# FFN output products of a hybrid decoder layer: sums of weight blocks and differences of token operands made in the first-product stage, kept in DRAM, and loaded ready

## The chip, the cores and the metric

One core of a Trainium2 chip runs the whole layer in one launch. The metric is the device time of an execution in microseconds (us), as the median of several runs. The engines are TensorE (PE, matmuls), VectorE (DVE), ScalarE (ACT), GpSimd (POOL) and SyncE (SP), whose queue issues the transfers spoken of here. Each engine works through its own instructions in a fixed order and waits on semaphores.

## The reference

The layer is two half-step SwiGLU feed-forward networks (FFNs) around a token mixer. The change touches the two FFNs alone.

```python
def swiglu(x, w_in, w_out):
    gate, up = jnp.split(x @ w_in, 2, axis=-1)
    return (jax.nn.silu(gate) * up) @ w_out

h = h + 0.5 * swiglu(rms_norm(h, ffn1_norm[i]), ffn1_w_in[i], ffn1_w_out[i])
h = h + hybrid_mixer(rms_norm(h, mix_norm[i]), ...)
h = h + 0.5 * swiglu(rms_norm(h, ffn2_norm[i]), ffn2_w_in[i], ffn2_w_out[i])
return rms_norm(h, final_norm)[:, N_META:]
```

D_MODEL is 1024, D_FF 2816, SEQ 1024, and 16 meta tokens stand ahead of the sequence, so the first FFN has 1040 columns of tokens and the second 1024. All is float32.

## The kernel before, in words

*Number format.* A float32 product is three matmuls on two-part numbers (`mm3`, L155 to L160: high by high, high by low, low by high). An operand is made by `split` (L135 to L138): ACT casts the high part (L136), then POOL or DVE subtracts it to get the low part (L137).

*Seven products for eight.* Every product of 2 x 2 blocks is done with seven block products (numbered 0 to 6 and run in the order 0, 1, 2, 3, 5, 4, 6), on sums and differences of weight blocks and of token blocks, which the adds to PSUM results turn into the four blocks of the output. The weight sums are four DVE instructions (`pair_weights`, L223, L224, L226, L227).

*First products.* For each f of 22 blocks of 128 D_FF columns, a block of w_in for the gate and one for the up part, both loaded as four 256 KB pieces (`load_half`, L145), are multiplied with the normalised tokens in seven products of two column groups (`hidden`, L277 to L319); f = 0 is done plainly (`hidden_plain`). DVE adds PSUM to kept parts (L284), ACT applies the silu, DVE multiplies gate and up (L287), and for f % 4 < 2 subtracts one result from the other (L290). The two halves are written to `hid_d` in DRAM (L292). 168 matmuls of 260 columns make a period of about 20 us. These stages lie at 60 to 505 us and 2416 to 2855 us of the span.

*Output products.* Four f make a group g, five groups in all; the last two blocks are done plainly behind them. For each group and each half e of the output's columns, four 256 KB blocks of w_out are loaded and `pair_weights` makes the seven weight operands; `output` (L377 to L401) runs seven products of four 260-column chains (or two of 512 in the second FFN), and after each product DVE adds the scaled PSUM to the residual `hT` (L398). The tiles `ps_start_gx`, `mm`, `px` and `rx` are these chains' PSUM banks. The token operands of the next group are made meanwhile by `operand_steps` (L347 to L371), a generator that takes one step after each product: `load_hidden` (L340 to L344) loads the group's hidden values into `lower` and `upper`, L360 makes three differences in two halves each (t2 on DVE, the two that follow on POOL), and `put` splits each of the seven operands in two halves, the low parts of operands 0, 2, 3, 4 on DVE, of 1, 5, 6 on POOL. The low part of a weight operand is made on POOL, that of product 2 on DVE. The stages lie at 505 to 735 us and 2856 to 3082 us.

*Order and buffers.* A scheduler puts each engine's instructions in an order at build time; the text of the program gives the dependencies. Raw weights, their high and their low parts have four buffers each, the big tiles of hidden values (`lower`, `upper`, tag `hid`) two, the small tiles of `hidden` (tag `tmp`) five. SP issues all transfers in its own fixed order.

Of the kernel before, what the change touches and what calls it, by code (L numbers as in the profile page):

```python
# [10 lines left out]
F32 = mybir.dt.float32  # L11
# [5 lines left out]
P = 128  # L17
# [28 lines left out]
def _cut(edges):  # L46
    return [(a, b - a) for a, b in zip(edges, edges[1:])]
# [49 lines left out]
def hybrid_layer(ctx, tc, a):  # L97
# [177 lines left out]
    def ffn(fp, hidp, hT, hn, slots, spare, second, w_in, w_out, hid_d, last_blocks, last_weights, tail, first, w0=None):  # L275

        def hidden(f, ws, order, after):  # L277
            sg, q3, q1, q2 = (fp.tile([P, 2, hn], F32, name=n, tag="tmp", bufs=5) for n in ("sg", "q3", "q1", "q2"))
            chains = [[None, None], [None, None]]
            view = hid_d[f].rearrange("p (g h n) -> p g h n", g=2, h=2)  # L280
            made = [0, 0]

# [39 lines left out]
        def hidden_plain(f, ws):  # L322
            view = hid_d[f].rearrange("p (g h n) -> p g h n", g=2, h=2)
# [13 lines left out]
            for half, x in enumerate((q3, q2)):  # L337
                SP.dma_start(view[:, :, half], x)

        def load_hidden(f):  # L340
            ts = [hidp.tile([P, 8 * hn], F32, name=n, tag="hid", bufs=2) for n in ("lower", "upper")]
            for i, t in enumerate(ts):
                SP.dma_start(t.rearrange("p (f t) -> p f t", f=2), hid_d[f + 2 * i:f + 2 * i + 2].rearrange("f p t -> p f t"))
            return ts  # L344


        def operand_steps(xs, ts, puts):  # L347
            b11, b21, t1, b22 = halves_of(ts)
            t2 = [fp.tile([P, 2, hn], F32, name="t2", tag="tmp", bufs=5) for _ in range(2)]
            part2 = lambda x, k: x[k.start // 2] if x is t2 else x[:, k]  # L350

            def put(i, src):
                eng = V if i in puts else G
                for k in (slice(0, 2), slice(2, 4)):
                    split(part2(src, k), xs[i][0][:, k], xs[i][1][:, k], eng)
                    yield i

            def minus(eng, out, x, y):
                for k in (slice(0, 2), slice(2, 4)):
                    eng.tensor_tensor(out=part2(out, k), in0=part2(x, k), in1=part2(y, k), op=ALU.subtract)  # L360
# [7 lines left out]
            yield from put(3, b11)  # L368
            yield from put(5, b21)
            yield from put(4, t1)  # L370
            yield from put(6, b22)  # L371
# [5 lines left out]
        def output(f, e, xs, steps):  # L377
            def block(fi, dh):
                c0 = (4 * dh + 2 * e) * P
                raw = wtile("wraw")  # L380
                SP.dma_start(raw.rearrange("p (f d) c -> p f (d c)", f=2),
                             w_out[0][(f + 2 * fi) * P:(f + 2 * fi + 2) * P, c0:c0 + 2 * P].rearrange("(f p) c -> p f c", p=P))
                return raw

            raws = [[block(fi, dh) for fi in range(2)] for dh in range(2)]
            chains = [{}, {}]
            for i, (wh, wl) in pair_weights(*raws, FAST[min(f // 4, 1)][e]):
# [16 lines left out]
        ng = NF // 4  # L404
        for f in range(NF):
            if f == 0:
                hidden_plain(f, w0 or plain_weights(w_in))
                second()
                continue
            after = lambda i: None  # L410
            if f == NF - 1:
                steps = operand_steps(slots[0], ts, PUTS[0])
# [5 lines left out]
            if f == NF - 3:  # L418
                ts = load_hidden(0)
        for g in range(ng):  # L420
            steps = operand_steps(slots[(g + 1) % 2], load_hidden(4 * g + 4), PUTS[1]) if g + 1 < ng else iter(())
# [6 lines left out]
        for q in range(4):  # L428
            s = slice(2 * hn * q, 2 * hn * q + 2 * hn)
            raw = fp.tile([P, 2, hn], F32, name="raw", tag="tmp", bufs=5).rearrange("p a n -> p (a n)")  # L430
            SP.dma_start(raw, hid_d[f0 + q // 2][:, 2 * hn * (q % 2):2 * hn * (q % 2 + 1)])
# [99 lines left out]
    hid1_d = tc.dram_tile([NF, P, T], F32, name="hid1_d")  # L531
# [56 lines left out]
    ffn(fp, hidp, hT, HN1, slots, spare, start_differences, a["ffn1_w_in"], a["ffn1_w_out"], hid1_d, MIX3[2:] + MIX3[:2], last_weights1, tail1,  # L588
# [875 lines left out]
    hid2_d = tc.dram_tile([NF, P, SEQ], F32, name="hid2_d")  # L1464

# [29 lines left out]
    ffn(fp, fp, hm, HN2, slots, spare, second2, a["ffn2_w_in"], a["ffn2_w_out"], hid2_d, _cut(range(0, SEQ + 1, 256)), last_weights2, tail2,  # L1495
# [24 lines left out]
```

## Time and profile before

| | us |
|---|---|
| median of 3 runs | 3123.21 (3118.93 to 3125.72) |
| the profiled execution | 3122.52 |
| its span, first to last instruction | 3120.7 |
| PE busy | 2940.9 (94%) |
| DVE busy | 1875.0 (60%) |
| POOL busy | 1665.4 (53%) |
| ACT busy | 1300.9 (42%) |

PE's share is an average over stages. The granted clock of PE, 0.969 in the mean, is the share of the higher of its two levels (2.4 and 1.2 GHz) that the records show. Where the text gives a time without "long", it is a point of the span in us. A number in brackets in a row of the timeline is the idle time of that engine just before, with what ended it.

### The profile page before, as it was taken

The page shows a single profiled execution, that of the slowest core. Times are in us where ns is not written, and L with a number is a line of the kernel's source. Part 1 is how long each engine was busy: PE and PEld are TensorE (multiplying, and loading weights), DVE is VectorE, ACT ScalarE, POOL GpSimd, SP SyncE. Part 2 cuts the span into 40 slices and gives each one's busy share as a digit, 9 for nine tenths or more (in the row PEclk, how much of TensorE's full clock was granted, in tenths as well). Part 3 has the DMA queues.
Part 4 walks back from the last instruction along what each step waited for, and adds up shares of the span by engine and source line. Part 5 has one row for each costly group of instructions (what it writes and reads, how often), then busy time and mean ns, then how long its engine had stood idle before and what let it go on. Part 6 is the DMA issues. An engine that isn't in the chain of part 4 may idle for free. (4 is left out here: it accounts for less than half of the span.)

```text
span 3120.7 us, 55266 instructions
## 1 busy us (share of the span) xinstructions
PE 2940.9 (94%) x21463; PEld 2773.9 (89%) x21463; DVE 1875.0 (60%) x3467; ACT 1300.9 (42%) x2687; POOL 1665.4 (53%) x1419
## 2 busy tenths in 40 slices
PE   7999998999899999988999989999998999999898
PEld 6999998899898899988889889988888999998677
DVE  8444448987755556465656665672438544447976
ACT  4333334333555545443445444453324433334332
POOL 5444447754566556543555445445526544447862
PEclk8999999999999999988999999989999999999999
DMA  2322223313222221211221222144533222223322
GB/s 91 106 79 82 79 77 110 115 49 105 57 62 62 61 57 50 71 41 57 71 54 55 65 71 59 58 141 125 185 110 112 80 91 82 80 80 102 113 64 88
DMA packets 324889, 257.19 MB, mean 82 GB/s; under 512 B 24961, under 2 KB 294530, under 8 KB 324626
## 3 DMA queue, kind: packets, MB, share of 16 engines
q1 hardware_dynamic: 324560, 253.65, 26.9%
q8 instruction: 168, 2.75, 0.4%
q14 instruction: 95, 0.78, 0.1%
q10 hardware_dynamic: 66, 0.02, 0.0%
HBM read 200.12 MB, written 53.49 MB: 81 GB/s over the span
## 5 line engine op out<-in xcount | busy, mean ns | idle before, releaser
L137 POOL TENSOR_TENSOR wl<-wraw,wh 128x512 fp32r<-128x512 f32 x806 | 1088.5, 1358 | 1125.3 <-ACT wh L136 1071.8
L136 ACT CAST wh<-wraw 128x512 fp32r<-128x512 f32 x864 | 535.5, 625 | 1040.5 <-issue 195.2
L983 DVE SCALAR_TENSOR_TENSOR cb<-raw,cw,cb 128x344 f32<-128x344 f32 (+2 forms) x216 | 140.1, 680 | 21.0 <-ACT cb L981 19.7
L158 PE MATMUL ps_gate_mm<-act,wh 128*128 128x344 f32 (+1 forms) x352 | 124.7, 355 | 5.0 <-DVE raw L610 4.4
L159 PE MATMUL ps_gate_mm<-act,wh 128*128 128x344 f32 (+1 forms) x352 | 115.6, 328 | 0.0
L160 PE MATMUL ps_gate_mm<-act,wl 128*128 128x344 f32 (+1 forms) x352 | 115.5, 329 | 0.0
L158 PE MATMUL ps_start_mm<-on,wh 128*128 128x260 f32 x392 | 111.7, 285 | 1.9 <-DVE hT L398 1.4
L158 PE MATMUL ps_ffn_mm<-on,wh 128*128 128x256 f32 (+1 forms) x376 | 111.2, 296 | 1.8 <-ACT wh L136 1.5
L160 PE MATMUL ps_start_mm<-on,wl 128*128 128x260 f32 x392 | 111.1, 283 | 1.8 <-POOL wl L137 1.8
L159 PE MATMUL ps_start_mm<-on,wh 128*128 128x260 f32 x392 | 110.9, 283 | 0.0
L160 PE MATMUL ps_ffn_mm<-on,wl 128*128 128x256 f32 (+1 forms) x376 | 110.2, 293 | 0.7 <-POOL wl L137 0.7
L159 PE MATMUL ps_ffn_mm<-on,wh 128*128 128x256 f32 (+1 forms) x376 | 109.8, 292 | 0.0
L284 DVE TENSOR_TENSOR q<-q,ps_start_px 128x260 f32<-128x260 f32 x42 | 17.7, 422 | 124.7 <-PE ps_start_px L160 124.6
L158 PE MATMUL ps_start_px<-on,wh 128*128 128x260 f32 x308 | 87.8, 285 | 4.0 <-DVE hT L398 2.1
L223 DVE TENSOR_TENSOR wraw<-wraw 128x512 f32<-128x512 f32 x62 | 52.5, 847 | 60.9 <-DMA wraw<-ffn_w_in 44.6
L158 PE MATMUL ps_start_mm<-ox,wh 128*128 128x260 f32 x292 | 84.2, 289 | 4.4 <-ACT ox L136 2.5
L160 PE MATMUL ps_start_px<-on,wl 128*128 128x260 f32 x308 | 88.0, 286 | 0.0
L159 PE MATMUL ps_start_px<-on,wh 128*128 128x260 f32 x308 | 87.8, 285 | 0.0
L159 PE MATMUL ps_start_mm<-ox,wh 128*128 128x260 f32 x292 | 83.6, 286 | 3.6 <-DVE ox L137 3.6
L160 PE MATMUL ps_ffn_px<-on,wl 128*128 128x256 f32 (+1 forms) x284 | 83.8, 295 | 0.8 <-POOL wl L137 0.8
L158 PE MATMUL ps_ffn_px<-on,wh 128*128 128x256 f32 (+1 forms) x284 | 83.5, 294 | 0.7 <-ACT wh L136 0.7
L160 PE MATMUL ps_start_mm<-ox,wl 128*128 128x260 f32 x292 | 83.7, 287 | 0.0
(1661 smaller groups left out, 11082.2 us busy)
## 6 DMA issues: line engine op xcount, KB each, us to landing
wraw<-ffn_w_in SPq DMA_DIRECT2D x176, 256.0 KB
wraw<-w_in SPq DMA_DIRECT2D x168, 256.0 KB
wraw<-ffn_w_out SPq DMA_DIRECT2D x88, 256.0 KB
wraw<-w_out SPq DMA_DIRECT2D x48, 256.0 KB
hid_d<-q SPq DMA_DIRECT2D x44, 260.0 KB
hid_d<-q SPq DMA_DIRECT2D x44, 256.0 KB
gates_d<-raw SPq DMA_DIRECT2D x16, 512.0 KB
wraw<-w_branch_ret SPq DMA_DIRECT2D x32, 256.0 KB
```

What stands on the lines that cost most here:

```text
L136: S.copy(hi, raw)
L137: (eng or G).tensor_tensor(out=lo, in0=raw, in1=hi.bitcast(F32), op=ALU.subtract)
L158: PE.matmul(ps, lhsT=wh, rhs=xh, start=first and i == 0, stop=False, skip_group_check=grow)
L159: PE.matmul(ps, lhsT=wh, rhs=xl, start=False, stop=False, skip_group_check=grow)
L160: PE.matmul(ps, lhsT=wl, rhs=xh, start=False, stop=last and i == n - 1, skip_group_check=grow)
L223: V.tensor_tensor(out=ru[0], in0=ru[0], in1=ru[1], op=ALU.add)
L284: V.tensor_tensor(out=out, in0=out, in1=ps, op=ALU.add)
L983: V.scalar_tensor_tensor(out=c, in0=raw[:, s0 + k:s0 + k + n], scalar=cw[:, 24 * k + ct:24 * k + ct + 1], in1=c, op0=ALU.mult, op1=ALU.add)
```

## The change

Each group's seven token operands and each half's four weight sums are made while the first products run, written to DRAM (`opnd_d`, `sums_d`), and loaded ready in the output stage. In blocks with f % 4 > 1, `hidden` loads two parts of the block f − 2 back into a tile `kept`, makes the three differences (t2 on DVE, b11 and d on POOL) and writes them. In even blocks from 2 to 20, `weight_sums` loads four blocks of w_out, makes the four sums on DVE (L383 to L386, the names `a21`, `a11`, `a12`, `a22`) and writes 1 MB. In the output stage, `load_operands` loads one pair of operands ahead of the pair that is being split, and `output` takes products 0, 1 and 5 from w_out and 2, 3, 4 and 6 from the stored sums. The line numbers of before and after answer to each other so: L284 to L295, L287 to L298, L290 to L301, L398 to L438.

```diff
+        ng = NF // 4
+        hid_d = tc.dram_tile([2, P, 4 * hn], F32, name=f"hid_d{hn}")
+        opnd_d = tc.dram_tile([7 * ng, P, 4 * hn], F32, name=f"opnd_d{hn}")
+        sums_d = tc.dram_tile([2 * ng, P, 16 * P], F32, name=f"sums_d{hn}")
...
         def hidden(f, ws, order, after):
...
+            kept = None
+            if 1 < f <= 4 * ng and f % 2 == 0:
+                sums = weight_sums((f - 2) // 2)
+            if f < 4 * ng and f % 4 > 1:
+                kept = hidp.tile([P, 8 * hn], F32, name="kept", tag="hid", bufs=2).rearrange("p (u n) -> p u n", u=4)
+                for u, i in enumerate((0, 4)):
+                    SP.dma_start(kept[:, u], part_of(f - 2, i))
...
                 if made[half] == 2:
-                    SP.dma_start(view[:, :, half], x)
+                    put_hidden(f, half, x)
+                    if half and kept is not None:
+                        flat = lambda t: t.rearrange("p g n -> p (g n)")
+                        b11, t1, t2, d = (kept[:, u] for u in range(4))
+                        V.tensor_tensor(out=t2, in0=flat(q2), in1=t1, op=ALU.subtract)
+                        SP.dma_start(part_of(f, 2), t2)
+                        G.tensor_tensor(out=b11, in0=t2, in1=b11, op=ALU.subtract)
+                        SP.dma_start(part_of(f, 3), b11)
+                        G.tensor_tensor(out=d, in0=flat(q3), in1=t2, op=ALU.subtract)
+                        SP.dma_start(part_of(f, 5), d)
 
             for i, grp in order:
+                if 1 < f <= 4 * ng and f % 2 == 0 and grp == 0:
+                    next(sums, None)
...
+        def weight_sums(n):
+            w = hidp.tile([P, 8 * hn], F32, name="sums", tag="hid", bufs=2)[:, :16 * P].rearrange("p (i c) -> p i c", i=4)
+            a11, a12, a21, a22 = (w[:, i] for i in range(4))
+            for i, (dh, fi) in enumerate(((0, 0), (0, 1), (1, 0), (1, 1))):
+                SP.dma_start(w[:, i].rearrange("p (f c) -> p f c", f=2), block(4 * (n // 2), n % 2, fi, dh))
+            yield
+            yield
+            yield V.tensor_tensor(out=a21, in0=a21, in1=a22, op=ALU.add)
+            yield V.tensor_tensor(out=a11, in0=a21, in1=a11, op=ALU.subtract)
+            yield V.tensor_tensor(out=a12, in0=a12, in1=a11, op=ALU.subtract)
+            V.tensor_tensor(out=a22, in0=a22, in1=a11, op=ALU.subtract)
+            SP.dma_start(sums_d[n], w.rearrange("p i c -> p (i c)"))
+            yield
...
+        LOADS = ((0, 1), (2, 3), (5, 4), (6,))
...
-            minus(V, t2, b22, t1)
-            yield from put(0, b11)
-            minus(G, b11, t2, b11)
-            yield from put(1, b21)
-            minus(G, b21, b21, t2)
-            yield from put(2, t2)
...
+        def operand_steps(xs, g, t, puts):
+            for n, pair in enumerate(LOADS):
+                ahead = load_operands(g, LOADS[n + 1]) if n + 1 < len(LOADS) else None
+                for u, i in enumerate(pair):
+                    eng = V if i in puts else G
+                    for k in (slice(0, 2), slice(2, 4)):
+                        split(t[:, u, k], xs[i][0][:, k], xs[i][1][:, k], eng)
+                        yield i
+                t = ahead
...
         def output(f, e, xs, steps):
...
+            def weights():
+                for i in (0, 1, 2, 3, 5, 4, 6):
+                    raw = wtile("wraw")
+                    if i in (0, 1, 5):
+                        SP.dma_start(raw.rearrange("p (f d) c -> p f (d c)", f=2), block(f, e, *{0: (0, 0), 1: (1, 0), 5: (1, 1)}[i]))
+                    else:
+                        j = {2: 0, 6: 1, 4: 2, 3: 3}[i]
+                        SP.dma_start(raw.rearrange("p k c -> p (k c)"), sums_d[idx][:, 512 * j:512 * j + 512])
+                    yield i, put_weights(raw, eng=V if i in FAST[min(f // 4, 1)][e] else None)
...
-            for i, (wh, wl) in pair_weights(*raws, FAST[min(f // 4, 1)][e]):
+            for i, (wh, wl) in weights():
```

DVE in the first products, before: an early block of the first FFN, `q` being the kept parts, `sg` the gate.

```order
L284 TENSOR_TENSOR sg<-sg,ps_start_px 128x260 x2
L284 TENSOR_TENSOR q_1416<-q_1416,ps_start_px 128x260
L287 TENSOR_TENSOR q_1416<-q_1416,sg 128x260
L223 TENSOR_TENSOR wraw<-wraw 128x512
L284 TENSOR_TENSOR q_1418<-q_1418,ps_start_mm 128x260
L224 TENSOR_TENSOR wraw<-wraw 128x512
L284 TENSOR_TENSOR q_1416<-q_1416,ps_start_px 128x260
L287 TENSOR_TENSOR q_1416<-q_1416,sg 128x260
```

The same place after, in the block f = 3; `sums` are w_out blocks.

```order
L295 TENSOR_TENSOR sg<-sg,ps_start_px 128x260 x2
L295 TENSOR_TENSOR q_1197<-q_1197,ps_start_px 128x260
L383 TENSOR_TENSOR sums<-sums 128x512
L298 TENSOR_TENSOR q_1197<-q_1197,sg 128x260
L223 TENSOR_TENSOR wraw<-wraw 128x512
L384 TENSOR_TENSOR sums<-sums 128x512
L295 TENSOR_TENSOR q_1199<-q_1199,ps_start_mm 128x260
L224 TENSOR_TENSOR wraw<-wraw 128x512
```

Two of the four weight sums now stand between the addition of product 5 (`q<-q,ps_px`) and the addition of product 4 (`q<-q,ps_mm`).

SP in the same blocks, before: each block's four weight loads and its two writes.

```order
L145 DMA wraw<-ffn_w_in 128x4x128 x4
L292 DMA hid_d<-q_2140 256x1x260
L292 DMA hid_d<-q_2142 256x1x260
L145 DMA wraw<-ffn_w_in 128x4x128 x4
L292 DMA hid_d<-q_2380 256x1x260
```

After, in the block f = 3 (L308, L310, L312 write the differences, L380 loads w_out, L387 writes the sums):

```order
L367 DMA opnd_d_364<-q_1940 128x520
L367 DMA opnd_d_364<-q_1942 128x520
L145 DMA wraw<-ffn_w_in 128x4x128
L308 DMA opnd_d_364<-kept 128x520
L310 DMA opnd_d_364<-kept 128x520
L312 DMA opnd_d_364<-kept 128x520
L145 DMA wraw<-ffn_w_in 128x4x128
L380 DMA sums<-ffn_w_out 128x2x256 x2
L145 DMA wraw<-ffn_w_in 128x4x128
L380 DMA sums<-ffn_w_out 128x2x256 x2
L145 DMA wraw<-ffn_w_in 128x4x128
L387 DMA sums_d_365<-sums 128x2048
```

The four loads of w_out have come between the three writes and the weight loads of the next block.

DVE in the output products, before, in one group of the first FFN (`t` is the difference t2; L223 and L224 are weight sums):

```order
L398 SCALAR_TENSOR_TENSOR hT<-ps_start_mm,hT 128x260
L360 TENSOR_TENSOR t_7407<-upper,lower 128x520
L360 TENSOR_TENSOR t_7408<-upper,lower 128x520
L398 SCALAR_TENSOR_TENSOR hT<-ps_start_px,hT 128x260
L398 SCALAR_TENSOR_TENSOR hT<-ps_start_mm,hT 128x260
L398 SCALAR_TENSOR_TENSOR hT<-ps_start_px,hT 128x260
L398 SCALAR_TENSOR_TENSOR hT<-ps_start_gx,hT 128x260
L398 SCALAR_TENSOR_TENSOR hT<-ps_start_mm,hT 128x260
L398 SCALAR_TENSOR_TENSOR hT<-ps_start_gx,hT 128x260
L398 SCALAR_TENSOR_TENSOR hT<-ps_start_px,hT 128x260
L223 TENSOR_TENSOR wraw<-wraw 128x512
L398 SCALAR_TENSOR_TENSOR hT<-ps_start_mm,hT 128x260
L224 TENSOR_TENSOR wraw<-wraw 128x512
```

After, in the same stage (L438 is the addition to the residual, `opnd` a loaded operand):

```order
L137 TENSOR_TENSOR ox<-opnd,ox 128x520
L438 SCALAR_TENSOR_TENSOR hT<-ps_start_mm,hT 128x260
L438 SCALAR_TENSOR_TENSOR hT<-ps_start_px,hT 128x260
L137 TENSOR_TENSOR ox<-opnd,ox 128x520
L438 SCALAR_TENSOR_TENSOR hT<-ps_start_gx,hT 128x260 x3
L438 SCALAR_TENSOR_TENSOR hT<-ps_start_rx,hT 128x260
L137 TENSOR_TENSOR oe<-opnd,oe 128x520
L438 SCALAR_TENSOR_TENSOR hT<-ps_start_mm,hT 128x260
L438 SCALAR_TENSOR_TENSOR hT<-ps_start_px,hT 128x260
L137 TENSOR_TENSOR oe<-opnd,oe 128x520
L438 SCALAR_TENSOR_TENSOR hT<-ps_start_mm,hT 128x260
```

The differences and the sums are gone from between the additions; the halves of operands that DVE splits stand there alone.

## Rows read from the trace of the kernel before

**Rows 1.** The trace by stretches: from:to, length, busy time of each engine (instructions), granted clock, DMA share, GB/s.

```profile
90.00:480.00 390.00, 389.69 (x3241) 389.10 (x3240) 181.16 (x292) 148.14 (x326) 176.40 (x135) 1.00 0.29 85
485.00:505.00 20.00, 17.45 (x138) 16.61 (x137) 16.56 (x18) 9.07 (x21) 18.72 (x12) 1.00 0.21 65
505.00:735.00 230.00, 210.70 (x1666) 206.18 (x1665) 198.49 (x375) 79.21 (x137) 156.39 (x105) 0.97 0.29 92
2440.00:2840.00 400.00, 399.35 (x3347) 399.15 (x3346) 182.47 (x302) 155.08 (x341) 186.60 (x143) 1.00 0.29 86
2840.00:3082.00 242.00, 221.07 (x943) 173.52 (x943) 197.59 (x249) 84.55 (x151) 171.70 (x114) 0.96 0.28 91
665.00:735.00 70.00, 70.00 (x587) 70.00 (x586) 51.75 (x119) 15.99 (x26) 30.12 (x24) 1.00 0.21 62
```

**Rows 2.** Waits from 505 to 735 us: line waiting, releaser, us in total, times, longest.

```profile
PE ps_start_gx L158 <- DVE hT L398: 8.6, 6, 2.7
...
PE ps_start_mm L158 <- DVE hT L398: 3.7, 6, 1.2
```

**Rows 3.** Timeline of PE: start, us, line, operation; in brackets the idle time before and its releaser.

```profile
555.22 0.39 PE L158 MATMUL ps_start_px<-on,wh 128*128 128x260 f32 x1 [0.92 <-DVE hT L398]
...
556.92 0.39 PE L158 MATMUL ps_start_mm<-on,wh 128*128 128x260 f32 x1 [1.19 <-DVE hT L398]
```

**Rows 4.** Timeline of DVE, the same microseconds.

```profile
553.36 1.47 DVE L223 TENSOR_TENSOR wraw<-wraw 128x512 f32<-128x512 f32 x1
...
555.09 1.43 DVE L137 TENSOR_TENSOR ox<-lower,ox 128x520 fp32r<-128x520 f32 x1
```

**Rows 5.** Shorter stretches, columns as in the first group.

```profile
505.00:665.00 160.00, 140.70 (x1081) 136.18 (x1080) 146.75 (x258) 63.22 (x111) 126.27 (x82) 0.96 0.33 105
...
505.00:520.00 15.00, 12.80 (x99) 11.95 (x98) 15.00 (x25) 9.26 (x18) 10.86 (x7) 1.00 0.65 213
580.00:595.00 15.00, 14.79 (x124) 14.58 (x123) 14.70 (x28) 7.34 (x13) 10.04 (x7) 1.00 0.11 36
```

**Rows 6.** DVE's groups, 485 to 735 us: count | busy us, mean ns | idle before.

```profile
L360 DVE TENSOR_TENSOR t<-upper,lower 128x520 f32<-128x520 f32 x9 | 11.1, 1265 | 1.4 <-DMA upper<-hid_d 1.4
L223 DVE TENSOR_TENSOR wraw<-wraw 128x512 f32<-128x512 f32 x10 | 10.7, 1071 | 9.8 <-DMA wraw<-ffn_w_out 9.7
L224 DVE TENSOR_TENSOR wraw<-wraw 128x512 f32<-128x512 f32 x10 | 10.2, 1017 | 0.0
...
L226 DVE TENSOR_TENSOR wraw<-wraw 128x512 f32<-128x512 f32 x10 | 8.9, 892 | 0.1
...
L227 DVE TENSOR_TENSOR wraw<-wraw 128x512 f32<-128x512 f32 x10 | 7.6, 759 | 0.0
```

**Rows 7.** POOL's groups in the same stretch.

```profile
L360 POOL TENSOR_TENSOR lower<-t,lower 128x520 f32<-128x520 f32 x10 | 16.7, 1673 | 0.0
L360 POOL TENSOR_TENSOR upper<-upper,t 128x520 f32<-128x520 f32 x10 | 16.1, 1607 | 0.7 <-DVE t L360 0.7
```

**Rows 8.** The view of line L226: ns shortest/median/longest, first and last start, form.

```profile
L226 DVE TENSOR_TENSOR wraw<-wraw x62: 676/1443/1794, 71.6 to 3060.6; 128x512 f32<-128x512 f32 x62
```

**Rows 9.** Timeline of DVE in one period of first products.

```profile
278.54 1.33 DVE L287 TENSOR_TENSOR q<-q,q 128x260 f32<-128x260 f32 x1 [1.03 <-ACT q L316]
...
282.63 0.43 DVE L284 TENSOR_TENSOR sg<-sg,ps_start_px 128x260 f32<-128x260 f32 x1 [2.41 <-ACT sg L302]
289.55 0.43 DVE L284 TENSOR_TENSOR q<-q,ps_start_px 128x260 f32<-128x260 f32 x1 [6.50 <-PE ps_start_px L160]
...
291.56 0.69 DVE L223 TENSOR_TENSOR wraw<-wraw 128x512 f32<-128x512 f32 x1 [1.12 <-DMA wraw<-ffn_w_in]
292.17 0.42 DVE L284 TENSOR_TENSOR q<-q,ps_start_mm 128x260 f32<-128x260 f32 x1
```

**Rows 10.** Timeline of PE there.

```profile
293.60 0.28 PE L158 MATMUL ps_start_mm<-ox,wh 128*128 128x260 f32 x1
```

**Rows 11.** SP's own waits from 100 to 500 us.

```profile
SPq L343 <- DMA hid_d<-q: 1.6, 1, 1.6
```

More of the change, by code (lines that the diff above doesn't have):

```diff
@@ L273, in plain_weights, with ffn @@
         return [put_weights(r) for rs in raw_pair(cols(w_in, 0), cols(w_in, DFF)) for r in rs]
-    def ffn(fp, hidp, hT, hn, slots, spare, second, w_in, w_out, hid_d, last_blocks, last_weights, tail, first, w0=None):
+    def ffn(fp, hidp, hT, hn, slots, spare, second, w_in, w_out, last_blocks, last_weights, tail, first, w0=None):
+        ng = NF // 4
+        hid_d = tc.dram_tile([2, P, 4 * hn], F32, name=f"hid_d{hn}")
+        opnd_d = tc.dram_tile([7 * ng, P, 4 * hn], F32, name=f"opnd_d{hn}")
+        sums_d = tc.dram_tile([2 * ng, P, 16 * P], F32, name=f"sums_d{hn}")
         def hidden(f, ws, order, after):
@@ L337, in hidden_plain @@
             for half, x in enumerate((q3, q2)):
[L338 to L360, printed above, removed]
-            minus(V, t2, b22, t1)
-            yield from put(0, b11)
-            minus(G, b11, t2, b11)
-            yield from put(1, b21)
-            minus(G, b21, b21, t2)
-            yield from put(2, t2)
[L368 to L371, printed above, removed]
@@ new lines, in hidden_plain, with part_of, put_hidden, block @@
+                put_hidden(f, half, x)
+        def part_of(f, i):
+            return opnd_d[7 * (f // 4) + i][:, 2 * hn * (f % 2):2 * hn * (f % 2 + 1)]
+        def put_hidden(f, half, x):
+            if f < 4 * ng:
+                SP.dma_start(part_of(f, (1, 6)[half] if f % 4 > 1 else (0, 4)[half]), x.rearrange("p g n -> p (g n)"))
+            else:
+                SP.dma_start(hid_d[f - 4 * ng].rearrange("p (g h n) -> p g h n", g=2, h=2)[:, :, half], x)
+        def block(f, e, fi, dh):
+            c0 = (4 * dh + 2 * e) * P
+            return w_out[0][(f + 2 * fi) * P:(f + 2 * fi + 2) * P, c0:c0 + 2 * P].rearrange("(f p) c -> p f c", p=P)
@@ new lines, in ffn, with load_operands @@
+        LOADS = ((0, 1), (2, 3), (5, 4), (6,))
+        def load_operands(g, pair):
+            t = hidp.tile([P, 8 * hn], F32, name="opnd", tag="hid", bufs=2).rearrange("p (u k n) -> p u k n", u=2, k=4)
+            for u, i in enumerate(pair):
+                SP.dma_start(t[:, u].rearrange("p k n -> p (k n)"), opnd_d[7 * g + i])
+            return t
+        def operand_steps(xs, g, t, puts):
+            for n, pair in enumerate(LOADS):
+                ahead = load_operands(g, LOADS[n + 1]) if n + 1 < len(LOADS) else None
+                for u, i in enumerate(pair):
+                    eng = V if i in puts else G
[3 more added lines that the diff above has]
+                t = ahead
@@ L377, in output @@
         def output(f, e, xs, steps):
[L378 to L385, printed above, removed]
+            idx = 2 * (f // 4) + e
+            def weights():
[3 more added lines that the diff above has]
+                        SP.dma_start(raw.rearrange("p (f d) c -> p f (d c)", f=2), block(f, e, *{0: (0, 0), 1: (1, 0), 5: (1, 1)}[i]))
+                    else:
+                        j = {2: 0, 6: 1, 4: 2, 3: 3}[i]
+                        SP.dma_start(raw.rearrange("p k c -> p (k c)"), sums_d[idx][:, 512 * j:512 * j + 512])
+                    yield i, put_weights(raw, eng=V if i in FAST[min(f // 4, 1)][e] else None)
             chains = [{}, {}]
-            for i, (wh, wl) in pair_weights(*raws, FAST[min(f // 4, 1)][e]):
+            for i, (wh, wl) in weights():
                 chain = i in (1, 3, 5)
@@ L417, in ffn @@
             hidden(f, dict(ffn_weights(w_in, f)), first if f == 1 else order, after)
-            if f == NF - 3:
-                ts = load_hidden(0)
+            if f == NF - 2:
+                ts = load_operands(0, LOADS[0])
         for g in range(ng):
-            steps = operand_steps(slots[(g + 1) % 2], load_hidden(4 * g + 4), PUTS[1]) if g + 1 < ng else iter(())
+            steps = operand_steps(slots[(g + 1) % 2], g + 1, load_operands(g + 1, LOADS[0]), PUTS[1]) if g + 1 < ng else iter(())
             for e in range(2):
@@ L1493, in tail2 @@
             SP.dma_start(a["out"][0][t * P:(t + 1) * P, :], ot)
[L1495 removed]
+    ffn(fp, fp, hm, HN2, slots, spare, second2, a["ffn2_w_in"], a["ffn2_w_out"], _cut(range(0, SEQ + 1, 256)), last_weights2, tail2,
         [(i, e) for i in (0, 1, 2, 3, 5, 4, 6) for e in (1, 0)], w0)
```

11 lines of the change are left out of this document (3 added, 8 removed).

## The prediction, made before the changed kernel had run

> **What bounds the kernel now.** I first read busy time by stretch, to see where TensorE (PE) is not working. In the FFNs' first products it is busy for 389.69 of 390 us and 399.35 of 400 us at full granted clock [rows 1]: there is nothing to win there, only something to lose. In the two output stages it is not: from 485 to 735 us PE is busy 17.45 of 20 and 210.70 of 230 us, from 2840 to 3082 us 221.07 of 242 us. That is 2.55 + 19.30 + 20.93 = 42.8 us of idle time. The granted clock is also below 1.00 there, 0.97 over 230 us and 0.96 over 242 us: 6.9 + 9.7 = 16.6 us in which work advanced at the 1.2 GHz level instead of 2.4. Together **59.4 us** is all that the change can return.
>
> Who is late there? PE's waits in the output stage are nearly all for the PSUM additions of L398 on VectorE (DVE): 8.6 us on gx, 3.7 us on mm [rows 2]. The timeline shows why. At 555.22 and 556.92 PE starts after 0.92 and 1.19 us of idle, each released by an addition; ahead of each addition, in DVE's queue, stands something else of 1.4 us: a sum of weight blocks (553.36, L223), then the low part of half an operand (555.09, L137) [rows 3, 4]. So PE waits for a short addition behind long SBUF work, and DVE is busy 146.75 of the 160 us from 505 to 665 [rows 5]. In the last two groups, where no operand is split any more, DVE is busy for 51.75 of 70 us, and PE never stops although the sums L223 to L227 are still made there [rows 1]. What stops PE is therefore the pile on DVE, not the sums as such.
>
> **The change part by part.**
>
> *Removed from the output stages.* Of DVE, in 485 to 735 us: 11.1 us of differences (L360) and 10.7 + 10.2 + 8.9 + 7.6 = 37.4 us of sums; of POOL: 16.7 + 16.1 = 32.8 us of differences [rows 6, 7]. The second FFN has the same instructions on 512-column blocks, as many again. From the 160 us that carry operands go all 11.1 us and about two thirds of the sums, 25 us: DVE falls from 147 to about 111 us. Fewer POOL operations also make what stays cheaper: the same sum takes 676 ns or 1443 ns, median 1443 [rows 8], and the long ones are those beside POOL's work.
>
> How much of the 59.4 us comes back? All of it if DVE is never late, which the last two groups show at a DVE share of 51.75/70 = 74%. DVE's 111 us in a stage cut to some 135 us is 82%, between that and the 92% of before; and from 580 to 595 us DVE is busy 14.70 of 15 us with PE at 14.79 [rows 5], so even a full DVE need not stop PE where additions stand between the long operations, as they do in the changed order (only halves of operands, with one to four additions between two of them, where two differences stood in a row and sums after single additions). I take 80%: **−48 us**. Bounds: −59.4, and −30 if the splits of operands alone (one of the two waits in [rows 3, 4]) keep half of the loss.
>
> *Added to the first products*: the same number of instructions on each compute engine, so all that left the output stages is now beside products that leave no gap. Per FFN, ten blocks f make t2 (DVE) and b11, d (POOL), and ten make four sums on DVE; SP gets 310 more transfers. Engine time is there: DVE is busy 181.16 of 390 us and POOL 176.40 [rows 1]; DVE's 48.5 us and POOL's 33 us raise both to under 60%. What costs is place, in order queues.
>
> (a) *Sums in the blocks f = 3, 7, 11, 15, 19* (five per FFN). In a period of before (286 to 299 us) DVE adds product 5 at 289.55, waits 1.12 us for the weights (L223 at 291.56), and at 292.17 adds product 4's PSUM, to 292.6 [rows 9]; PE starts product 6 in that PSUM at 293.60 [rows 10]. The slack is 1.0 us. In the changed order L383, which waits for weight loads of its own, stands between the first of these and all the others, and L384 too stands ahead of the addition. When do its blocks land? Their buffer is the one that t2, b11 and d are written from, so they wait for these three writes. t2 can be made when the block's last gating has ended, at 278.54 + 1.33 = 279.9 in this period [rows 9], then 1.3 us; b11 and d follow on POOL with 1.6 to 1.7 us each [rows 7] between pairs of weight splits: d is ready at some 286.5 us. From there the queue has to move the write of d, the four loads and the weights between them, about 7 x 256 KB = 1.84 MB. The fastest stretch of the trace moved 213 GB/s at a share of 0.65 [rows 5], 328 GB/s if full: 5.6 us, to 292.1. Even before, with four transfers in that time, DVE waited until 291.56 for the weights [rows 9]. L383 of 0.7 to 1.4 us, L298, L223 and L384 then put the addition's end at 294.5 to 297 instead of 292.6, against a limit of 293.6: 1 to 3.5 us late. I take 2 us, ten times: **+20 us** (0, if the loads are there by 291; 40, if each also meets the longer sums and a landing 2 us later).
>
> (b) *Sums in f = 1, 5, 9, 13, 17*: loaded in time, but four in a row between the two gate additions, 4 x 0.68 to 4 x 1.44 us [rows 8]. Between these two additions DVE idles 2.41 us, to 282.63 [rows 9], which nearly covers 2.7 us and leaves 3.4 us of 5.8; the second one frees a PSUM bank that PE's product 3 needs. I take 0.7 us ten times: **+7** (0 to 20).
>
> (c) At the start of each FFN the first loads stand ahead of the next block's weights on SP: about one transfer of 256 KB each, **+2** (0 to 6).
>
> (d) t2 on DVE in front of the next block's gate addition, b11 and d on POOL in front of weight splits: POOL has 214 us of gaps in 390 [rows 1], over 10 us of each block. **0** (to 5).
>
> (e) *Transfers in the output stage*: operands come ready made, seven a group of 512 or 520 KB instead of two loads of 1 MB, so some 7.3 MB per group (with 3.5 MB of weights) instead of 4.1 (2 + 2): in some 40 us 185 GB/s. The trace moved 213 at 0.65 busy [rows 5], so the queue holds it, and a pair is asked for one pair (some 11 us) ahead: **0** (to 15, one late pair per group).
>
> A load of kept operands needs what an earlier block wrote. The trace has one such wait on SP, 1.6 us in the first products of the first FFN [rows 11], where nothing close reads what was just written; the new loads read a block two back, some 40 us old. The Trainium skill (DMA: Bandwidth & Descriptors, "Rules for kernel authors") has a dependent transfer issued only after the first one's completion, on the same queue too. By this rule SP stands still when a write is slow, and all later weight loads with it: it speaks against the change, and is what the third rival prices from rows.
>
> Sum: −48 + 20 + 7 + 2 = −19 us against the profiled execution's 3122.5 us (span 3120.7 us): 3103.5; it lies 0.7 us below the median of the runs, 3123.2, so **3104 us**.
>
> One rule makes the gain doubtful from the other side: the long sums. The median 1443 against 676 ns [rows 8] appear wherever POOL works on SBUF. The Trainium skill (SBUF — State Buffer, "Who interferes with whom") has DVE and GpSimd share one pair of ports under an exclusive lock. By it a sum costs as much in its new place, and the sum above would only move within the range of (b).
>
> **The rivals.**
>
> 1. *The loads land in time* (first products keep their 389.69 of 390). For it: DMA share there is 0.29 [rows 1]; against it: the slack of 1.0 us. Gain −48, costs 0 to 2: **3076 us**. Chance 0.20.
>
> 2. *DVE stays the bound of the output stage*: operand halves and additions, which all remain, keep half the loss: −30, and first products cost 29: **3122 us**, no change. For it: one of the two waits in [rows 3, 4] stands behind half an operand. Against: 580 to 595 us. Chance 0.18.
>
> 3. *SP and DVE hold each other up in the first products*, slower. If L383's loads come 2 us later than in (a), because SP waits for the three writes and holds the next weights too, each of the ten late blocks loses 4 us and each of the ten early ones 2: +60 + 2, and with −48 it is +14; with a gain of −42 it is +20. It decides from 4.8 us lost in each late block without any other loss. **3140 us**. For it: seven transfers between d and the sum, against four before; against it, that the share of 0.29 leaves room. Chance 0.14.
>
> 4. *It does not do what it says*: the counts of instructions per engine are equal before and after, so work is moved, not saved; if DVE in the output stage were not the limit (PE waiting for weights) nothing would return. PE's largest waits are not for weights [rows 2]. Chance 0.03, 3135 us.
>
> **How the numbers follow.** My forecast, costs in part as large as in (a) and (b), 3090 to 3115 us: 0.45. This kernel's measurement can tell some 0.2% (6 us) from no change: faster is below 3117, slower above 3129.5. Faster: 0.45 + 0.20 and a small part of rival 2, 0.67. Within: most of rival 2, 0.16. Slower: rivals 3 and 4, 0.17. The range reaches from 3068 (rival 1 with a little less than the full 59.4 back) to 3133 (between rivals 2 and 3); left out are the full gain at no cost, and rival 3 at its price.
>
> **What would show it.** Right: in the output stages PE busy over 97% with the clock at 0.99; waits for the line of the PSUM addition below 4 us; in the first products gaps of about 2 us every fourth block, released by the addition of product 4's PSUM behind L383, with DVE waiting for a transfer. Without such gaps rival 1 holds; with DVE over 90% busy in the output stage and PE waiting as before, rival 2; with gaps of 4 us and more that end in weights from SP, rival 3. Wrong altogether would be idle PE in the output stages that ends in operand transfers.

## The result, and the profile after

The changed kernel takes 3145.43 us (median of 4 runs, 3144.29 to 3146.3) against 3121.07 us before (4 runs, 3111.08 to 3125.72): a ratio of 1.0082, 95% interval 1.006 to 1.0103. It is 0.8% slower. I had forecast 3104 us and a range of 3068 to 3133 us.

Where the time went is told by the stages. First products run from their first addition in the trace (L284 before, L295 after) to the first addition of the output products (L398, L438), and these to the end of their last addition on gx.

| stage, us | before | after | difference |
|---|---|---|---|
| first products, FFN 1 | 427.2 | 461.8 | +34.6 |
| output products, FFN 1 | 229.1 | 205.7 | −23.4 |
| between the two | 1695.6 | 1692.5 | −3.1 |
| first products, FFN 2 | 426.3 | 470.3 | +44.0 |
| output products, FFN 2 | 226.5 | 197.8 | −28.7 |

Stage times here and below are those of one profiled execution of each kernel. The output stages gave back 52.1 us. The first products took 78.6 us. With the 3.1 us between the two that makes 23.4, the difference of the two spans (3144.0 and 3120.7 us). The view by stretches of the changed kernel (columns as in [rows 1]):

```profile
90.00:480.00 390.00, 367.60 (x2971) 363.38 (x2970) 190.84 (x315) 134.75 (x301) 185.84 (x143) 0.98 0.46 149
...
545.00:735.00 190.00, 186.33 (x1539) 184.68 (x1537) 147.58 (x303) 69.12 (x121) 115.47 (x82) 1.00 0.51 169
2440.00:2840.00 400.00, 371.58 (x2983) 366.69 (x2984) 184.24 (x317) 136.70 (x307) 192.66 (x144) 0.97 0.46 147
2908.00:3106.00 198.00, 194.75 (x849) 157.26 (x848) 140.10 (x188) 74.79 (x132) 118.22 (x87) 1.00 0.52 173
```

In the output stages PE is now busy for 186.33 of 190 us at a full clock, where it was 210.70 of 230 at 0.97. In the first products it is busy for 367.60 of 390 us, where it was 389.69, and the granted clock there is 0.98 and 0.97 where it was 1.00. DMA moves 149 GB/s where it moved 85. What PE waits for in FFN 1, from 60 to 545 us and then from 545 to 746 us:

```profile
PE ps_start_mm L158 <- DVE q L295: 20.9, 12, 3.8
PE ps_start_px L158 <- DVE sg L295: 7.8, 6, 1.9
```

```profile
PE ps_start_mm L158 <- DVE hT L438: 2.1, 2, 1.9
PE ps_start_gx L158 <- DVE hT L438: 1.5, 4, 0.5
```

The wait for the residual's additions has fallen from 8.6 and 3.7 us [rows 2] to 1.5 and 2.1. A wait for the addition of product 4's PSUM has come, 20.9 us. The longest of these gaps, on PE, DVE, SP and POOL:

```profile
226.04 0.39 PE L158 MATMUL ps_start_mm<-ox,wh 128*128 128x260 f32 x1 [3.85 <-DVE q L295]
```

```profile
217.98 0.43 DVE L295 TENSOR_TENSOR q<-q,ps_start_px 128x260 f32<-128x260 f32 x1 [6.50 <-PE ps_start_px L160]
223.41 0.69 DVE L383 TENSOR_TENSOR sums<-sums 128x512 f32<-128x512 f32 x1 [5.00 <-DMA wraw<-ffn_w_in]
224.02 0.42 DVE L298 TENSOR_TENSOR q<-q,sg 128x260 f32<-128x260 f32 x1
224.36 0.69 DVE L223 TENSOR_TENSOR wraw<-wraw 128x512 f32<-128x512 f32 x1
224.96 0.68 DVE L384 TENSOR_TENSOR sums<-sums 128x512 f32<-128x512 f32 x1
225.56 0.42 DVE L295 TENSOR_TENSOR q<-q,ps_start_mm 128x260 f32<-128x260 f32 x1
```

```profile
211.71 0.32 SPq L312 DMA_DIRECT2D opnd_d<-kept  x1
212.96 0.38 SPq L145 DMA_DIRECT2D wraw<-ffn_w_in  x1
216.12 0.90 SPq L380 DMA_DIRECT2D sums<-ffn_w_out  x2
217.12 0.42 SPq L145 DMA_DIRECT2D wraw<-ffn_w_in  x1
217.59 1.01 SPq L380 DMA_DIRECT2D sums<-ffn_w_out  x2
218.64 0.47 SPq L145 DMA_DIRECT2D wraw<-ffn_w_in  x1
```

```profile
211.64 2.54 POOL L137 TENSOR_TENSOR wl<-wraw,wh 128x512 fp32r<-128x512 f32 x2
```

Read from below. POOL has freed the weight buffers by 214.2 us, but SP stands from 213.3 to 216.1 at L380, whose buffer is held by the write L312; so the third weight load leaves only at 217.12. Six transfers of 256 KB then leave within 3 us. DVE waits for the last of them until 223.41 with L383 at the head of its queue, and the addition that PE needs comes at 225.56. PE is idle for 3.85 us. And then, in the stretches around the gap:

```profile
218.00:222.00 4.00, 4.00 (x35) 3.98 (x34) 0.41 (x1) 0.62 (x1) 0.49 (x2) 1.00 0.94 294
222.00:224.00 2.00, 0.19 (x2) 0.00 (x0) 0.59 (x1) 0.00 (x0) 1.15 (x1) 1.00 0.38 114
224.00:226.00 2.00, 0.00 (x0) 0.00 (x0) 2.00 (x6) 0.00 (x0) 0.00 (x0) 1.00 0.00 0
226.00:228.00 2.00, 1.96 (x10) 1.96 (x11) 2.00 (x4) 0.62 (x1) 0.64 (x1) 0.59 0.00 0
228.00:230.00 2.00, 2.00 (x12) 2.00 (x12) 2.00 (x5) 0.39 (x1) 0.93 (x1) 0.55 0.76 319
230.00:232.00 2.00, 2.00 (x18) 2.00 (x18) 0.76 (x2) 0.00 (x0) 0.00 (x0) 1.00 0.86 342
```

The DMA engines are 0.94 busy from 218 to 222 us, while DVE waits and PE still works; from 224 to 226 us, while PE waits for DVE, they move nothing. For 4 us after the gap the granted clock is 0.59 and 0.55, which is 1.7 us more. Ten and twelve matmuls run in 2 us where eighteen do a moment later.

The period shown is the extreme one. Such a gap stands in ten blocks, five in each FFN, and it is 3.1 to 3.9 us long in all of them, but SP's wait at L380 is 2.7 us only here and 0.9 us in the mean of the other four blocks of FFN 1 (waits of SP from 60 to 545 us):

```profile
SPq L292 <- DMA opnd_d<-q: 39.1, 18, 4.3
...
SPq L380 <- DMA opnd_d<-kept: 6.4, 5, 2.7
```

Another of the ten, on SP and DVE, with its gap on PE:

```profile
397.36 0.37 SPq L145 DMA_DIRECT2D wraw<-ffn_w_in  x1
```

```profile
398.35 0.43 DVE L295 TENSOR_TENSOR q<-q,ps_start_px 128x260 f32<-128x260 f32 x1 [6.50 <-PE ps_start_px L160]
401.99 0.69 DVE L383 TENSOR_TENSOR sums<-sums 128x512 f32<-128x512 f32 x1 [3.22 <-DMA wraw<-ffn_w_in]
...
405.21 0.41 DVE L295 TENSOR_TENSOR q<-q,ps_start_mm 128x260 f32<-128x260 f32 x1
```

```profile
405.68 0.39 PE L158 MATMUL ps_start_mm<-ox,wh 128*128 128x260 f32 x1 [3.13 <-DVE q L295]
```

The same load before:

```profile
288.57 0.37 SPq L145 DMA_DIRECT2D wraw<-ffn_w_in  x1
```

Before, the last weight load left 1.0 us ahead of product 5's addition (289.55 [rows 9]), the first sum began 3.0 us after the load had left (291.56), and product 4's addition began 0.6 us after that. Here the load left 1.0 us ahead too, but the first sum began 4.6 us after it, and product 4's addition 3.2 us after that, behind L383, L298, L223 and L384. In the mean of the ten blocks product 4's addition comes 4.5 us later than before: 0.6 us because the last weight load leaves later, 1.6 us because it lands more slowly (read from the start of the sum that waits for it), and 2.4 us by what stands on DVE between the first sum and the addition.

### The profile page after: what moved, and what is told of

Its sections match the earlier page's. It is cut to its first block, busy times and chain, and to the rows that moved or that the text cites. A ratio compares the mean times of both kernels' runs of the same rounds, so it can differ in the third digit from the quotient of the medians.

```text
span 3144.0 us, 55888 instructions
## 1 busy us (share of the span) xinstructions
PE 2940.9 (94%) x21463; PEld 2779.0 (88%) x21463; DVE 1832.4 (58%) x3467; ACT 1291.0 (41%) x2687; POOL 1641.1 (52%) x1419
## 5 line engine op out<-in xcount | busy, mean ns | idle before, releaser
L298 DVE TENSOR_TENSOR q<-q,q 128x260 f32<-128x260 f32 (+1 forms) x84 | 63.6, 757 | 55.7 <-ACT q L338 55.7
L158 PE MATMUL ps_ffn_mm<-ox,wh 128*128 128x256 f32 (+1 forms) x264 | 77.6, 294 | 17.1 <-DVE q L295 16.9
```

The source lines that it names most:

```text
L158: PE.matmul(ps, lhsT=wh, rhs=xh, start=first and i == 0, stop=False, skip_group_check=grow)
```

## The experiments

Two theories stood against each other. **H**: a sum that waits for its loads stands on DVE ahead of PSUM additions. **T**, later **C**: the weights of the first products themselves come late, because other transfers stand ahead of them on SP and on the DMA engines; the first sum of these weights, L223, also stands ahead of product 4's addition. All ratios are to the kernel before, run on the same chip in turn. First products are given as FFN 1 / FFN 2, in us.

**The sums on DVE left out.** The edit removes the four DVE instructions and keeps their loads and their write.

```diff
-            yield V.tensor_tensor(out=a21, in0=a21, in1=a22, op=ALU.add)
-            yield V.tensor_tensor(out=a11, in0=a21, in1=a11, op=ALU.subtract)
-            yield V.tensor_tensor(out=a12, in0=a12, in1=a11, op=ALU.subtract)
-            V.tensor_tensor(out=a22, in0=a22, in1=a11, op=ALU.subtract)
+            yield
```

> The changed kernel without the four sums on DVE (L383 to L386); their loads and writes and everything else stay, so product operands 2, 3, 4 and 6 of the weights are unsummed blocks. In the changed kernel the first products last 461.8 us (FFN1) and 470.3 us (FFN2) where they lasted 427.2 and 426.3. Theory H (a sum that waits for its loads stands in DVE's queue ahead of PSUM additions): the stalls go, 428 to 434 us each, total 3066 to 3080 us. Theory T (the added transfers, 152 against 85 GB/s, make the weights of the first products late by themselves): stays at 455 to 470 us each, total above 3130 us.

Measured: 3124.74 us, ratio 1.0014 (1.000 to 1.0028); first products 449.2 / 454.8. Neither theory alone: 28 of the 78.6 us went, 50 stayed. (The profiled execution is the fastest of ten, 12 us below the median; by the medians some 21 us went.) DVE at one of the gaps that stayed:

```profile
212.35 0.43 DVE L295 TENSOR_TENSOR q<-q,ps_start_px 128x260 f32<-128x260 f32 x1 [6.50 <-PE ps_start_px L160]
...
218.23 0.69 DVE L223 TENSOR_TENSOR wraw<-wraw 128x512 f32<-128x512 f32 x1 [4.99 <-DMA wraw<-ffn_w_in]
218.84 0.42 DVE L295 TENSOR_TENSOR q<-q,ps_start_mm 128x260 f32<-128x260 f32 x1
```

No sum stands here, and DVE waits the same 5 us: now L223 waits, for weights, where it waited 1.12 us before [rows 9].

**Each half of the change alone.** First the operand differences, with `pair_weights` back in the output stage; then the weight sums alone, with `load_hidden` and the differences as before.

```diff
-            for i, (wh, wl) in weights():
+            for i, (wh, wl) in pair_weights(*raws, FAST[min(f // 4, 1)][e]):
```

> The operand differences are moved as in the change, the weight sums are made in the output stage as before. Theory H: first products as before, 427 to 431 us each; the output stages (229.1 and 226.5 us before, 205.7 and 197.8 changed) get back about a third to a half of 52 us, since 11 us of DVE and 33 us of POOL leave each but 37 us of sums stay on DVE: total 3095 to 3108 us. Theory T: the three writes and two loads of the kept parts make a part of the stalls, first products 440 us or more each, total 3120 us or more.

Measured: 3089.05 us, ratio 0.9903 (0.9887 to 0.9919); first products 427.7 / 432.6, output stages 216.3 / 201.7. The differences alone cost 7 us in the first products, 6 of them in FFN 2, and give back 37.6 us, more than the expected third to half of 52.

> Only the weight sums are moved, as the change moves them; operands and differences are as before. Theory H: sums wait for their loads in DVE's queue here too, but no write of differences holds their buffer, so the stalls are smaller than in the changed kernel: first products 435 to 455 us each; output stages give back some 30 us together: total 3105 to 3140 us. Theory T: the sums' 2 MB per two blocks are most of the added traffic, so first products are as in the changed kernel, 455 to 470 us each, total 3150 us.

Measured: 3119.72 us, ratio 0.9993 (0.9978 to 1.0008); first products 431.3 / 435.5, output stages 222.8 / 216.9. The sums alone cost 13 us and give 16: no change. So the halves cost 7 and 13 us in the first products, and together 78.6: what makes the loss is that they meet. Alone, each has the two big buffers and SP to itself; together, a load of one waits in SP's queue for a write of the other, as L380 does above. These two runs do not show that this is the reason; the next ones move the queues' order.

**The sums moved on DVE.** All work and all transfers of the change, but the four sums are pinned behind the second gate addition of the odd block.

```diff
                     add(sg[:, grp], ps)
                     S.activation(sg[:, grp], sg[:, grp], AF.Silu)
+                    if f % 2 and grp and sums:
+                        next(sums.pop())
...
+                tc.keep_in_program_order(V.tensor_tensor(out=out, in0=x, in1=y, op=op))
```

> The changed kernel with one thing moved: the sums of an even block are made one block later, in DVE's queue behind the second gate addition of the odd block, where DVE waits 6.5 us for PE; their loads are issued in the even block as before, some 20 us ahead of their use. All work and all transfers stay. Theory H: first products 428 to 440 us each (what is left comes from weights that SP issues late behind the new waits), total 3070 to 3090 us. Theory T: as the changed kernel, 455 us or more each, total above 3130 us.

Measured: 3131.23 us, ratio 1.0041 (1.0028 to 1.0054); first products 451.4 / 462.1. Theory H alone falls: with no sum in the way, DVE waits 47.2 us for weights in FFN 1 from 90 to 480 us (21.8 us before), and the same group of loads stands between the weight loads on SP.

**The w_out loads behind the same block's weights.** The kernel above, with the four loads pinned on SP.

```diff
-                SP.dma_start(w[:, i].rearrange(...), block(4 * (n // 2), n % 2, fi, dh))
+                tc.keep_in_program_order(SP.dma_start(w[:, i].rearrange(...), block(4 * (n // 2), n % 2, fi, dh)))
```

> As the kernel with the sums moved behind the second gate addition (first products 451.4 and 462.1 us), and in addition SP issues the four w_out loads of a block behind the four weight loads of that block, so that in every fourth block they no longer stand between these. Theory C (weights of the first products come late because other transfers stand ahead of them on SP and on the DMA engines, and DVE's first sum of these weights, L223, stands ahead of product 4's PSUM addition): the gaps of 2.4 to 2.7 us once in four blocks go, first products 435 to 446 us each, total 3095 to 3115 us; the loads of kept parts still stand ahead of two weight loads in another of four blocks. Theory H (only sums on DVE hold PE up): no change against 451 and 462, total 3131 us.

Measured: 3105.16 us, ratio 0.995 (0.9933 to 0.9967); first products 438.9 / 445.2. Theory C as expected: in FFN 1 the gaps of 2.2 to 2.7 us once in four blocks are gone, and gaps of 0.6 to 1.8 us stay, mostly in another of four blocks.

**Small transfers.** The kernel without sums on DVE, with loads of 32 of 256 columns and a write of 32 of 512; the output stage loads blocks of w_out in place of the stored ones.

```diff
-                SP.dma_start(w[:, i].rearrange("p (f c) -> p f c", f=2), block(...))
+                SP.dma_start(w[:, i].rearrange("p (f c) -> p f c", f=2)[:, :, :32], block(...)[:, :, :32])
```

> As the kernel without the sums on DVE (first products 449.2 and 454.8 us), and in addition the four loads of w_out and the write in the first products carry 32 of 256 columns, with the same waits on SP in the same places; the output stage takes unsummed blocks of w_out in place of the stored ones. Two forms of theory C: if bytes are what makes the weights late, first products fall to 428 to 434 us each and the total to 3070 to 3080 us; if SP's wait for the writes that hold the shared buffer is it, 440 us or more each remain and the total stays above 3100 us. With a part by each, 434 to 440 us.

Measured: 3104.81 us, ratio 0.9951 (0.9936 to 0.9965); first products 444.6 / 445.1. SP and the stretches at one gap:

```profile
211.23 0.42 SPq L145 DMA_DIRECT2D wraw<-ffn_w_in  x1
211.70 1.01 SPq L380 DMA_DIRECT2D sums<-ffn_w_out  x2
214.73 0.53 SPq L386 DMA_DIRECT2D sums_d<-sums  x1
215.30 0.63 SPq L145 DMA_DIRECT2D wraw<-ffn_w_in  x1
```

```profile
214.00:216.00 2.00, 2.00 (x19) 2.00 (x18) 0.00 (x0) 0.00 (x0) 0.00 (x0) 1.00 0.05 8
216.00:218.00 2.00, 1.18 (x10) 0.97 (x9) 0.00 (x0) 0.62 (x1) 1.12 (x1) 1.00 0.71 157
```

From 214 to 216 the DMA engines are 0.05 busy, and still the last weight load leaves only at 215.30: SP stands at the write L386 until its four loads have landed. So waits in SP's queue alone make weights late. The totals do not price the bytes: with small transfers the scheduler put L386 ahead of the last weight load, behind which it stands in the kernel without the sums, and this is a wait of its own, so 444.6 may not be set against 449.2 as a share. The timelines show what the bytes do: in the ten late blocks the first sum begins 3.1 to 4.1 us after the last weight load has left, against 4.9 to 6.0 us in the kernel without the sums, where the transfers have their full size.

**Everything behind the next block's weights.** Work and transfers as in the change. The next block's four weight loads are written ahead of the middle of this block; the loads of kept parts, the loads of w_out and the write of the sums are pinned behind them on SP, and the sums on DVE as above.

```diff
+                if i == 3 and grp == order[-2][1]:
+                    if f + 1 < NF:
+                        raws.append(raw_pair(cols(w_in, (f + 1) * P), cols(w_in, DFF + (f + 1) * P)))
+                    if f % 2 and sums:
+                        next(sums.pop())
...
+                            tc.keep_in_program_order(SP.dma_start(kept[:, u], part_of(f - 2, j)))
...
+            tc.keep_in_program_order(SP.dma_start(sums_d[n], w.rearrange("p i c -> p (i c)")))
```

> All work and all transfers of the changed kernel, but the loads of kept parts, the loads of w_out and the write of the sums stand on SP behind all four weight loads of the next block, and the four sums stand on DVE behind the second gate addition of the odd block. Theory C: first products 428 to 436 us each, output stages 205 and 198 us as in the changed kernel, total 3068 to 3085 us, faster than the kernel with the operand differences alone (3089 us). If the bytes as such are too many (150 against 85 GB/s), first products stay at 445 us or more and the total above 3110 us.

Measured: 3080.66 us, ratio 0.987 (0.9856 to 0.9885), faster than both kernels and than the differences alone; first products 428.2 / 430.4, output stages 209.8 / 197.5. SP in one period, and the stretches of the first products:

```profile
221.33 4.41 SPq L145 DMA_DIRECT2D wraw<-ffn_w_in  x3
225.79 2.04 SPq L387 DMA_DIRECT2D sums<-ffn_w_out  x4
```

```profile
90.00:480.00 390.00, 388.07 (x3211) 385.97 (x3210) 224.40 (x333) 146.40 (x324) 209.99 (x155) 1.00 0.51 166
...
2440.00:2840.00 400.00, 397.64 (x3305) 394.59 (x3303) 227.36 (x345) 154.93 (x342) 217.26 (x160) 1.00 0.52 171
```

The weight loads leave with nothing between them, and the loads of w_out after them. DMA moves 166 and 171 GB/s, more than the 149 and 147 of the changed kernel, and PE is busy for 388 of 390 us. The bytes were never too many; their place was wrong.

**The same, with the sums where the scheduler wants them on DVE.** This takes the pin from the four sums and nothing else.

```diff
-                tc.keep_in_program_order(V.tensor_tensor(out=out, in0=x, in1=y, op=op))
+                V.tensor_tensor(out=out, in0=x, in1=y, op=op)
```

> As the kernel with all added transfers behind the next block's weights on SP (first products 428.2 and 430.4 us, total 3080.7 us), but the four sums are put on DVE where the scheduler wants them: in the first FFN at the end of the block whose middle issued their loads, ahead of the last addition of product 4. So weights come on time and only the sums' place on DVE is bad again. Theory H as a second cause of its own: DVE waits 2 to 5 us for w_out blocks in front of that addition, ten times in each FFN, first products 445 to 470 us each, total 3110 to 3160 us. If only the weights' lateness mattered (theory C alone): as before the edit, 428 to 434 us each, 3080 to 3088 us.

Measured: 3115.3 us, ratio 0.9991 (0.9977 to 1.0006); first products 455.0 / 441.4. DVE at one place:

```profile
215.70 0.69 DVE L223 TENSOR_TENSOR wraw<-wraw 128x512 f32<-128x512 f32 x1 [3.25 <-DMA wraw<-ffn_w_in]
...
218.01 0.41 DVE L291 TENSOR_TENSOR q<-q,ps_start_px 128x260 f32<-128x260 f32 x1
...
242.94 0.90 DVE L390 TENSOR_TENSOR sums<-sums 128x512 f32<-128x512 f32 x1 [0.81 <-DMA sums<-ffn_w_out]
243.76 0.41 DVE L291 TENSOR_TENSOR q<-q,ps_start_mm 128x260 f32<-128x260 f32 x1
```

```profile
218.57 0.36 PE L158 MATMUL ps_start_px<-ox,wh 128*128 128x260 f32 x1 [0.89 <-DVE q L291]
...
220.82 0.48 PE L158 MATMUL ps_start_mm<-on,wh 128*128 128x260 f32 x1 [1.03 <-DVE q L291]
```

The edit costs 27 and 11 us, and the total came out as theory H expected, but not by its mechanism. A sum does stand ahead of product 4's addition (242.94), with a wait for w_out of 0.8 us and not of 2 to 5; but PE does not stop there: after 220.82 its next stop is 0.48 us at 248.57. Its stops for additions are at 218.57 and 220.82 and at the same places in every fourth block of FFN 1, where no sum of w_out is in the way. There the order of other instructions has changed with the pin: L223, which waits 3.25 us for the weights, and L224 stand ahead of both additions of product 5, where both stood behind the first of these in the kernel above. In FFN 1's first products PE's idle time is 17.5 us against 5.8, and the granted clock is 0.98 from 90 to 480 us where it was 1.00 in the run above; the two make up most of the 27 us. So this run does not show the place of the sums as a cause by itself. What shows it is the run without the sums, and a row from the start of FFN 2 in the next section.

Along the kernels with the same work and the same transfers, the sums moved on DVE return 18.6 of the 78.6 us, the w_out loads behind the same block's weights another 29.4, and all added transfers behind the next block's weights another 25.5: 73.5 in all. What remains is 5 us.

## Why the prediction was wrong, step by step

- **The bound, and what the output stages return.** Right. 48 us of 59.4 forecast, 52.1 measured, by the mechanism named: the wait for the residual's additions went, the clock rose to 1.00. Its makeup was not as I had it: I reckoned mostly with the sums (37 of 48 us of DVE), but the differences alone give 37.6 us and the sums alone 16. DVE's 11 us of differences and POOL's 33 us weigh more than 37 us of sums, which [rows 1] had hinted at: in the last groups the sums are made and PE does not stop.
- **(a), the sums in every fourth block.** This term failed by its size: 20 us forecast, 34 us of gaps measured. The place was right: the gap is on product 6, behind the addition of product 4, behind L383. I took 2 us of gap, and it is 3.1 to 3.9 us in each of the ten blocks. The step in it that was wrong: "from there the queue has to move ... 5.6 us, to 292.1", which is 2.5 us after product 5's addition. Measured, the first sum began 3.6 to 5.4 us after it, 4.1 in the mean. I had seen that the loads wait for the writes, but let the weights behind them go out as before. In the period shown first, SP stood 2.8 us at L380 and the last weight load left 1.6 us later than before; in the mean of the ten it left 0.6 us later, and it landed 4.6 us after it had left, not 3.0. What follows on DVE I had listed rightly: 1 to 3.5 us late was my bracket, and I took 2 where 3.4 came. (The 213 GB/s from which I had the 328 were not the fastest of the trace, which moved 349 GB/s from 2102 to 2117 us; the rate is not what failed.)
- **The clock.** This term was put at nothing, without a reason, though I had counted the clock among the gains. The gap of 3.85 us is followed by 4 us at 0.59 and 0.55. Over 390 and 400 us a clock of 0.98 and 0.97 is 7.8 + 12 = 20 us, as much as I had set for all of (a). (The 16.6 us among the gains are what the clock cost; the time at the lower level was twice that. The sum does not change.)
- **(b), the early sums.** Right in size, 5.5 us of gaps against 7, but not as described: "loaded in time" was wrong. From 258 to 263 us L383 waited 4.21 us for w_out, and PE then stood 1.1 to 1.2 us in four such blocks of FFN 1, and 0.4 to 0.6 us in two of FFN 2.

```profile
259.27 0.69 DVE L383 TENSOR_TENSOR sums<-sums 128x512 f32<-128x512 f32 x1 [4.21 <-DMA sums<-ffn_w_out]
```

- **(c), the start of each FFN.** FFN 1 shows no gap of its own there. FFN 2 has one of 4.13 us, against 2 us forecast for both. It is not late weights: L383 waits 9.10 us for w_out, and the additions of products 5 and 4 stand behind it. Here a sum that waits for its loads stops PE by itself, as in theory H.

```profile
2454.37 1.69 DVE L383 TENSOR_TENSOR sums<-sums 128x512 f32<-128x512 f32 x1 [9.10 <-DMA sums<-ffn_w_out]
...
2458.01 0.41 DVE L295 TENSOR_TENSOR q<-q,ps_ffn_mm 128x256 f32<-128x256 f32 x1
```

- **(d) and (e).** (e) at nothing was right: operands came in time, and the output stages' DMA share is 0.51 and 0.52. (d) is bounded by the kernel with the differences alone: its first products are 7 us longer, against 0 (to 5).
- **What no term had.** In another of four blocks PE stops as well, 8.6 us in all, because weights come late there too. At 271.75 it stops for 2.14 us; in that block SP had stood 4.3 us at the load of a kept part. With (a), (b) and (c) these gaps are nearly all of the 53 us by which PE's idle time in the first products grew; the clock makes most of the rest of the 78.6.
- **The rivals.** The third, slower, at 3140 us, came nearest, and its mechanism is in the trace: SP waits for the writes and holds the next weights. I gave it 0.14 because the share of DMA is 0.29. That share is an average over a stage; in the 4 us that decide, it is 0.94 (the row from 218 to 222 us above), and SP's wait does not show in it at all. That its sum came near was in part luck: it set 60 us for the late and early blocks, where 40 us of gaps were measured, and had neither the clock nor the other blocks. The first rival, 3076 us, is near what the change gives once the transfers and the sums are put in the right order: 3080.66.
- **The rule on dependent transfers.** By the Trainium skill (DMA: Bandwidth & Descriptors, "Rules for kernel authors") a transfer that reads what an earlier one wrote is issued only after the first one's completion. Waits of its kind are in the trace: SP stood 39.1 us in FFN 1 at loads of kept parts, L292, 18 times and at most 4.3 us. In the longest gap it was a neighbour: SP stood 2.8 us for a buffer that a write had not yet finished reading.

What stays open: how the loss divides between SP's waits and the bytes in front of the weights, beyond the means of the ten blocks, since the one run that made the transfers small also moved a wait; and what the sums' place alone would cost with the weights on time, since the run that was to show it changed the order of other instructions too.

## What to carry to other kernels

Work that moves into a stage without slack is priced by its place in each in-order queue, not by its time: for every queue ask which instruction can wait there, and what stands behind it. A transfer that waits for a buffer must not stand ahead of a transfer that feeds the busy engine, and a computation that waits for a load must not stand ahead of a short addition that frees PSUM. If two parts share buffers, try each alone: here one was worth 1.0%, the other nothing, both together cost 0.8%, and with the order put right both were worth 1.3%.

## What was not expected of the hardware

A gap on PE can cost more than itself: after 3.85 us without matmuls the granted clock was 0.59 and 0.55 for the next 4 us. It need not: after the 3.13 us ahead of 405.68 the clock stayed at 1.00. The DMA engines carried 166 to 171 GB/s through the first products without a loss on PE, and came to 294 GB/s at a share of 0.94 with six 256 KB transfers in flight, when DVE could use the last of them 4.8 us after its issue (218.64 to 223.41).
